# Attention heads: softmax weights left undivided, and each head's output multiplied by its rows' inverse sums

## The chip, the cores and the metric

The kernel runs on one core of a Trainium2 chip. The metric is the device time of one execution in microseconds. Engines are called PE (TensorE, matmuls), DVE (VectorE), ACT (ScalarE), POOL (GpSimd) and SP (SyncE, which issues the DMAs).

## What is computed

The reference is a network of several blocks on 512 tokens of width 1024, all in fp32. Three of its parts are attention: a block with 8 heads, which comes twice (two layers), and one with 16 heads of width 64. In each the part that matters here is a softmax over a row of scores, followed by the product with the values:

```python
s = jnp.where(mask[None, None], s, NEG_INF)
p = jax.nn.softmax(s, axis=-1).astype(v.dtype)
outs.append(jnp.einsum('bhqk,bhkd->bhqd', p, v[:, :kend]))
...
sc = jnp.einsum('bhqd,bhkd->bhqk', qb, kb).astype(jnp.float32) * scale + bias
sc = jnp.where(valid, sc, -jnp.inf)
p = jax.nn.softmax(sc, axis=-1).astype(vb.dtype)
return jnp.einsum('bhqk,bhkd->bhqd', p, vb)
```

## The kernel before

Activations lie feature by token (128 partitions of features, 512 tokens along the free dimension). Matmul operands are split into a high and a low fp32r half (`split`), so that a product takes three matmuls (`mm3`, L151 to L153). The stages follow one another: `mix` (heads and other branches), `ffn`, `mix`, `ffn`, `recurrent`, `mlp`, `attention`, `mlp`. The heads stand in `mix` (8 heads each) and in `attention` (16 heads), and both call `heads` with a list of items and a generator `filler`, which yields other matmuls (branches in `mix`, projections and output GEMMs in `attention`).

A head has four blocks of 128 queries, `qb` 0 to 3, with 128, 256, 384 and 512 keys. `scores` makes a block's scores in PSUM (L279 or L281, tag `ps_s`, two buffers), masks them, finds the row maximum (L291; in `attention` L295, which adds the bias too), and lets ACT take the exponent with the row sum as an accumulated by-product `sm` (L292, L297). Then it divides: DVE takes the reciprocal (L298), and the weights are multiplied by it row by row, the largest block on ACT (L300), the other three on DVE (L302). Here queries lie on the partitions, so the factor is one value per partition.

`turn` comes two blocks later (`depth` 2). It transposes a block of weights on PE (L314) into PSUM (tag `ps_t`, two buffers), and splits it (ACT L109, DVE L110). After the fourth block it multiplies by the values (L325, tag `ps_o`, one buffer): the two halves of the value operand give the two parts of the output in two halves of the partitions, so ACT copies one (L329, into `of`) and `done` adds it to the other (L523 in `mix`, L1030 in `attention`, where ACT and POOL then split it). Now queries lie along the free dimension. In `mix`, `of` has one buffer, shared with `prep`, which makes the queries of a later head (L509 writes `of`).

`prep` is called when block 1 of the head before has been scored, so just behind the `turn` of the fourth block of the head before that. In `attention` it calls `doubled` twice, each a product on DVE (`two`, L949) and four transposes into `ps_t` (L953); one is read by ACT and DVE as keys (`kh`, `kl`), one as queries (L963, L965).

`spread` (L199 to L205) is there before: it turns per-token columns into rows that are the same on all partitions, by transposing a column broadcast to 128x128 (L203, tag `ps_t`). The norms use it. The instructions of each engine are put in order ahead of time by a scheduler with a model of time; `high_priority` favours `scores` and `turn`, and `issue_after` holds instructions behind a given one.

Of the kernel before, what the change touches and what calls it, by code (L numbers as in the profile page):

```python
# [10 lines left out]
F32 = mybir.dt.float32  # L11
F32R = mybir.dt.float32r
I32 = mybir.dt.int32
AF = mybir.ActivationFunctionType
ALU = mybir.AluOpType
# [3 lines left out]
P = 128  # L19
# [47 lines left out]
class Net:  # L67
    def __init__(self, ctx, tc, d, out):
        self.tc, self.nc, self.d, self.out = tc, tc.nc, d, out
        self.small = ctx.enter_context(tc.tile_pool(name="small", bufs=1))  # L70
        self.base = ctx.enter_context(tc.tile_pool(name="base", bufs=1))
        self.psum = ctx.enter_context(tc.tile_pool(name="psum", bufs=1, space=PSUM))
        self.prm = self.small.tile([P, NPRM], F32, name="prm")

        self.half = self.small.tile([P, 32], F32, name="half")
        self.nc.gpsimd.memset(self.half[:, :16], -0.5)
        self.tab = self.small.tile([P, NTAB], F32, name="tab")
        self.uid = 0
        self.wide = 0
        self.after = []  # L80
# [189 lines left out]
    def scores(self, it, qb):  # L270
        nc = self.nc
        w = (qb + 1) * P
        s = self.ps("s")
        qs = slice(qb * P, w)
        q, k, rows = it["q"], it["k"], it.get("rows")
        if rows is None:

            for a, n in zip(k, range(2)):
                nc.tensor.matmul(out=s[:, :w], lhsT=q[:, qs], rhs=a[:, :w], start=n == 0, stop=n == 1)  # L279
        else:  # L280
            self.mm3(s[:, :w], (q[0][rows, qs], q[1][rows, qs]), (k[0][rows, :w], k[1][rows, :w]), True, True)  # L281
        bias = it.get("bias")
        if bias is None:
            nc.vector.memset(s[0:64, w - 64:w], NEG)
        else:
            pass
        m = self.t(self.small, "mx", 6, (P, 1))
        p = self.t(it["pool"], "p", it.get("p", 3))
        sm = self.t(self.small, "sm", 6, (P, 1))
        if bias is None:  # L290
            nc.vector.reduce_max(out=m, in_=s[:, :w], axis=AX, negate=True)  # L291
            nc.scalar.activation(out=p[:, :w], in_=s[:, :w], func=AF.Exp, bias=m, accum_out=sm)  # L292
        else:

            nc.vector.tensor_tensor_reduce(out=p[:, :w], in0=s[:, :w], in1=bias[:, 512 - w:], scale=-1.0,  # L295
                                           scalar=3e38, op0=ALU.add, op1=ALU.min, accum_out=m)
            nc.scalar.activation(out=p[:, :w], in_=p[:, :w], func=AF.Exp, bias=m, scale=-1.0, accum_out=sm)  # L297
        nc.vector.reciprocal(out=sm, in_=sm)  # L298
        if qb == 3:
            nc.scalar.activation(out=p, in_=p, func=AF.Copy, scale=sm)  # L300
        else:
            nc.vector.tensor_scalar(out=p[:, :w], in0=p[:, :w], scalar1=sm, scalar2=None, op0=ALU.mult)  # L302
        return p

    def turn(self, it, qb, p):

        nc = self.nc
        if qb == 0:
            it["pt"] = self.pair(it["pool"], "pt", 1, (P, 13, P))
        pth, ptl = it["pt"]  # L310
        pt = self.ps("t")
        for kb in range(qb + 1):
            ks = slice(kb * P, (kb + 1) * P)
            self.mark = nc.tensor.transpose(out=pt[:, ks], in_=p[:, ks], identity=self.c("ident"))  # L314

        dst = slice(qb, qb + 3 * qb + 1, 3)
        src = pt[:, :(qb + 1) * P].rearrange("p (k c) -> p k c", c=P)
        self.split((pth[:, dst], ptl[:, dst]), src)
        if qb == 3:

            o = self.ps("o")
            for kb in range(4):
                bs = slice(4 * kb, 4 * kb + 4 - kb)
                for pt in (pth, ptl):
                    nc.tensor.matmul(out=o[:, kb * P:], lhsT=it["v"](kb), rhs=pt[:, bs],  # L325
                                     start=kb == 0 and pt is pth, stop=kb == 3 and pt is ptl)
            a, b = (slice(0, 64), slice(64, 128))[::it["step"]]
            f = self.t(it["pool"], "of", it.get("of", 1))
            nc.scalar.activation(out=f[a], in_=o[b], func=AF.Copy)  # L329
            it["done"](o[a], f[a], a)  # L330

    def heads(self, items, filler, total, marks=None, hi=1000, depth=2):

# [29 lines left out]
        while pend:  # L363
            fill()
            turn()
            fill()
# [4 lines left out]
    def mix(self, l, gnext):  # L371
        nc, tc, d = self.nc, self.tc, self.d
        V, S_, G = nc.vector, nc.scalar, nc.gpsimd
# [4 lines left out]
        aout = [self.t(mp, "aout", 4) for _ in range(4)]  # L378
# [3 lines left out]
        with tc.tile_pool(name=f"att{l}", bufs=1, reuse_waits="tile") as ap:  # L382
# [28 lines left out]
            for j, S in enumerate((Sq, Sk)):  # L411
                for i in range(4):
                    nc.tensor.matmul(out=ps[:, 4 * j + i:4 * j + i + 1], lhsT=S[:, i * P:(i + 1) * P],
                                     rhs=self.c("inv", j, j + 1), start=True, stop=True)
# [25 lines left out]
            for i in range(4):  # L440
                f = vv[i // 2][:, i % 2 * 256:i % 2 * 256 + 256]
# [6 lines left out]
            for i in range(4):  # L448
                s = slice(i * 256, (i + 1) * 256)
                self.split((vn[0][:, s], vn[1][:, s]), vv[i // 2][:, i % 2 * 256:i % 2 * 256 + 256],  # L450
                           scale=r2[:, i:i + 1])
# [7 lines left out]
            for j in (6, 7):  # L459
                w = chunk(j)  # L460
# [28 lines left out]
            def values(j):  # L489
                wv = self.load(d["w_v"][l, j], P, pool=hp, tag="q", cap=384, raw_bufs=1, bufs=2)  # L490
                v = val[j] = self.t(ap, "v", 2, (P, 4, 4, 64), F32R)
                ps = self.ps("mm", (P, 4, P))
                for i in range(4):
                    ts = slice(i * P, (i + 1) * P)
                    self.mm3(ps[:, i], (ckv[0][:, ts], ckv[1][:, ts]), wv, True, True)
                self.split((v[:, :, 0::3], v[:, :, 1:3]), ps.rearrange("p i (h c) -> p i h c", c=64))
# [22 lines left out]
            def item(hd):  # L519
                j = hd // 2  # L520

                def done(o, f, rows):
                    V.tensor_tensor(out=aout[j][rows], in0=o, in1=f, op=ALU.add)  # L523
                    if hd in (0, 2, 4):
                        values(hd // 2 + 1)
                return dict(hd=hd, step=1 - hd % 2 * 2, rows=ALLP, pool=hp, prep=prep, done=done,
                            v=lambda kb: val[j][:, kb, hd % 2 * 2:hd % 2 * 2 + 2])
# [64 lines left out]
        with tc.tile_pool(name=f"gate{l}", bufs=1, reuse_waits="tile") as gp:  # L592
# [13 lines left out]
            for i in range(KT):  # L606
                m = self.t(gp, "m", 2)
                wo = None
                for n, nm in enumerate("cbda"):
# [4 lines left out]
                    if nm == "a":  # L614
                        w = self.load(d["w_br"][l, i, :, 768:], 512)
                    else:
                        wo = wo or self.load(d["w_br"][l, i, :, :768], 768)
                        w = (wo[0][:, n * 256:n * 256 + 256], wo[1][:, n * 256:n * 256 + 256])
# [284 lines left out]
    def attention(self, gnext):  # L903
        nc, tc, d = self.nc, self.tc, self.d
        V, S_, G = nc.vector, nc.scalar, nc.gpsimd
        xs, r = self.norm.xs, self.norm.r
        with tc.tile_pool(name="att", bufs=1, reuse_waits="tile") as ap:
            gqk = self.t(self.small, "rv", 1, (P, 4))[:, :1]
            V.scalar_tensor_tensor(out=gqk, in0=self.c("q_norm"), scalar=0.125, in1=self.c("k_norm"),
                                   op0=ALU.mult, op1=ALU.mult)  # L910
# [46 lines left out]
            def stacked(it, keys, queries, h):  # L957

                kk = self.t(ap, "kh", 3, dt=F32R), self.t(ap, "kl", 3, dt=F32R)
                self.split(kk, doubled(keys, h))  # L960
                q = self.t(ap, "q", 3, dt=F32R)
                ps = doubled(queries, h)
                S_.activation(out=q, in_=ps, func=AF.Copy, scale=gqk)  # L963
                lo = slice(64, P)
                V.scalar_tensor_tensor(out=q[lo], in0=ps[lo], scalar=gqk[lo], in1=q[lo].bitcast(F32), op0=ALU.mult,  # L965
                                       op1=ALU.subtract)
                it["k"], it["q"] = kk, q
# [46 lines left out]
            def item(hd):  # L1014
                group, h = groups[hd // 4], hd % 4

                def prep(it):
                    stacked(it, group[0][0], group[1][0], h)
                    b = bias[hd % 2]
                    nc.sync.dma_start(out=b[:, 256:], in_=d["bias"][hd])  # L1020
                    G.tensor_scalar(out=b[:, 256:], in0=b[:, 256:], scalar1=b[:, 256:257], scalar2=None,
                                    op0=ALU.subtract)
                    G.memset(b[0:64, 448:], NEG)
                    it["bias"] = b

                def done(o, f, rows):
                    j = hd // 2
                    if hd % 2 == 0:
                        os_[j] = self.pair(ap, "o", 6) if j < 6 else self.pair(ap, "k", 3)
                    V.tensor_tensor(out=f, in0=o, in1=f, op=ALU.add)  # L1030
                    self.split((os_[j][0][rows], os_[j][1][rows]), f, eng=G)

                return dict(p=4, step=1 - h % 2 * 2, pool=ap, prep=prep, done=done,
                            v=lambda kb: group[2][0][:, kb, h // 2, h % 2 * 2:h % 2 * 2 + 2])
# [177 lines left out]
```

## Time and profile before

| | us |
|---|---|
| median of 3 runs | 2803.64 |
| lowest and highest | 2803.21, 2806.1 |
| the profiled execution | 2796.84 |
| its span, first to last instruction | 2795.1 |
| PE busy in it | 2719.6 |
| DVE busy | 1570.9 |
| ACT busy | 1148.8 |
| POOL busy | 443.4 |

The span is what the profile's rows divide up; the profiled execution's own time is 1.7 us longer. Busy times of engines overlap. A row of waits names the engine and line that waited, then the line whose end released it, the time in total, how often, and the longest. The granted clock is 1.00 where PE runs at 2.4 GHz and 0.50 where it runs at 1.2 GHz.

### The profile page before, as it was taken

The numbers are of one execution on the slowest core, as the hardware profiler recorded it, in microseconds if no ns is written. First come the engines' busy times: TensorE is split into PE (matmuls) and PEld (weight loads), VectorE is DVE, ScalarE is ACT, GpSimd is POOL, SyncE is SP. The second block draws the span as 40 slices with busy tenths as digits, with TensorE's granted clock in tenths as the row PEclk, the third lists the DMA queues.
The fourth block names the chain that finished last, engine by engine and source line by source line (L and its number), as shares of the span: only waits on it lengthen the run. The fifth ranks groups of instructions, "written<-read, shape, count | busy, mean of one in ns | idle before, by whom it ended". The sixth has DMA issues, their size and how long they took to land.

```text
span 2795.1 us, 34599 instructions
## 1 busy us (share of the span) xinstructions
PE 2719.6 (97%) x13616; PEld 2304.5 (82%) x13616; DVE 1570.9 (56%) x2420; ACT 1148.8 (41%) x1894; POOL 443.4 (16%) x350
## 2 busy tenths in 40 slices
PE   8999999999999999999999998999999999899999
PEld 7778889888898778888888886888888888788887
DVE  5875555534467865456344478744444688744443
ACT  5553234322255543234222358433323567533222
POOL 5401110100004211101000100100004674200000
PEclk9999999999999999999999999999999999999999
DMA  4213232233322123242333322233223211133322
GB/s 152 63 46 98 92 106 89 91 100 96 96 89 95 48 64 98 93 132 64 95 96 100 92 93 78 77 106 97 94 96 97 72 63 63 63 98 92 105 95 87
DMA packets 77348, 249.70 MB, mean 89 GB/s; under 512 B 8577, under 2 KB 14593, under 8 KB 77185
## 3 DMA queue, kind: packets, MB, share of 16 engines
q1 hardware_dynamic: 77184, 247.49, 27.7%
q8 instruction: 107, 1.75, 0.3%
q14 instruction: 57, 0.46, 0.1%
HBM read 245.36 MB, written 2.10 MB: 89 GB/s over the span
## 4 chain that ended last, share of the span: by engine, by line
PE 88%; DVE 7%; ACT 3%; issue 1%; DMA 0%; POOL 0%; SPq 0%; DVEq 0%; ACTq 0%
PE ps_mm L151 16%; PE ps_mm L152 16%; PE ps_mm L153 16%; PE ps_s L152 9%; PE ps_s L151 9%; PE ps_s L153 9%; PE ps_o L153 3%; PE ps_o L152 3%; PE ps_o L151 3%; PE ps_o L325 1%; PE ps_t L314 1%; PE ps_s L279 1%; DVE xl L237 1%; ACT wh L109 1%; DVE S L214 0%
## 5 line engine op out<-in xcount | busy, mean ns | idle before, releaser
L109 ACT ACTIVATE wh<-raw 128x1024 fp32r<-128x1024 f32 (+3 forms) x403 | 411.8, 1024 | 1178.8 <-PE ps_mm L152 458.0
L110 DVE TENSOR_TENSOR wl<-raw,wh 128x1024 fp32r<-128x1024 f32 (+3 forms) x403 | 514.8, 1279 | 164.8 <-ACT wh L109 155.0
L151 PE MATMUL ps_mm<-xh,wh 128*128 128x512 f32 x1160 | 453.8, 392 | 7.3 <-ACT xh L112 6.8
L152 PE MATMUL ps_mm<-xl,wh 128*128 128x512 f32 x1160 | 453.2, 391 | 0.5 <-DVE xl L113 0.5
L153 PE MATMUL ps_mm<-xh,wl 128*128 128x512 f32 x1160 | 452.7, 391 | 0.0
L151 PEld LDWEIGHTS ps_mm<-xh,wh 128*128 128x128 f32 x1160 | 218.4, 188 | 53.8 <-ACT xh L112 6.8
L152 PEld LDWEIGHTS ps_mm<-xl,wh 128*128 128x128 f32 x1160 | 218.5, 188 | 45.4 <-DVE xl L113 1.0
L153 PEld LDWEIGHTS ps_mm<-xh,wl 128*128 128x128 f32 x1160 | 218.3, 188 | 45.4
L153 PE MATMUL ps_s<-xh,wl 128*128 128x512 f32 x552 | 215.5, 390 | 0.0
L151 PE MATMUL ps_s<-xh,wh 128*128 128x512 f32 x552 | 215.1, 390 | 0.0
L152 PE MATMUL ps_s<-xl,wh 128*128 128x512 f32 x552 | 214.8, 389 | 0.0
L151 PE MATMUL ps_mm<-hh,wh 128*128 128x512 f32 (+1 forms) x422 | 161.2, 382 | 0.0
L152 PE MATMUL ps_mm<-hl,wh 128*128 128x512 f32 (+1 forms) x422 | 160.9, 382 | 0.0
L153 PE MATMUL ps_mm<-hh,wl 128*128 128x512 f32 (+1 forms) x422 | 160.9, 382 | 0.0
L690 POOL TENSOR_TENSOR a<-a,rb 128x512 f32<-128x512 f32 x44 | 60.2, 1371 | 534.2 <-DVE a L689 534.2
L624 POOL TENSOR_TENSOR m<-m,g 128x512 f32<-128x512 f32 x48 | 62.6, 1304 | 433.4 <-DVE g L623 433.3
L153 PEld LDWEIGHTS ps_s<-xh,wl 128*128 128x128 f32 x552 | 103.6, 188 | 22.3 <-DVE wl L110 0.9
L151 PEld LDWEIGHTS ps_s<-xh,wh 128*128 128x128 f32 x552 | 103.7, 188 | 21.4
L152 PEld LDWEIGHTS ps_s<-xl,wh 128*128 128x128 f32 x552 | 103.6, 188 | 21.4
L151 PE MATMUL ps_s<-hh,wh 128*128 128x512 f32 (+1 forms) x308 | 117.0, 380 | 0.0
L152 PE MATMUL ps_s<-hl,wh 128*128 128x512 f32 (+1 forms) x308 | 116.8, 379 | 0.0
L153 PE MATMUL ps_s<-hh,wl 128*128 128x512 f32 (+1 forms) x308 | 116.8, 379 | 0.0
(462 smaller groups left out, 5858.4 us busy)
## 6 DMA issues: line engine op xcount, KB each, us to landing
raw<-in_w_in SPq DMA_DIRECT2D x96, 512.0 KB, 3.5
raw<-in_w_gu SPq DMA_DIRECT2D x88, 512.0 KB, 3.5
raw<-in_w_down SPq DMA_DIRECT2D x80, 512.0 KB, 3.5
raw<-in_w_up SPq DMA_DIRECT2D x64, 512.0 KB, 3.5
raw<-in_w_down SPq DMA_DIRECT2D x32, 448.0 KB, 3.3
raw<-in_w_qkv SPq DMA_DIRECT2D x24, 512.0 KB, 3.4
raw<-in_w_out SPq DMA_DIRECT2D x16, 512.0 KB, 3.5
raw<-in_a_w_in SPq DMA_DIRECT2D x16, 512.0 KB, 3.6
```

What stands on the lines that cost most here:

```text
L109: a = nc.scalar.activation(out=h, in_=src, func=AF.Copy)
L110: b = (eng or nc.vector).tensor_tensor(out=l, in0=src, in1=h.bitcast(F32), op=ALU.subtract)
L151: mm(out=ps, lhsT=a[0], rhs=b[0], start=first, stop=False)
L152: mm(out=ps, lhsT=a[0], rhs=b[1], start=False, stop=False)
L153: self.multiplied = mm(out=ps, lhsT=a[1], rhs=b[0], start=False, stop=last)
L237: lambda: self.nc.vector.scalar_tensor_tensor(out=l, in0=x, scalar=g, in1=h.bitcast(F32), op0=ALU.mult, op1=ALU.subtract))
L279: nc.tensor.matmul(out=s[:, :w], lhsT=q[:, qs], rhs=a[:, :w], start=n == 0, stop=n == 1)
L314: self.mark = nc.tensor.transpose(out=pt[:, ks], in_=p[:, ks], identity=self.c("ident"))
L325: nc.tensor.matmul(out=o[:, kb * P:], lhsT=it["v"](kb), rhs=pt[:, bs], start=kb == 0 and pt is pth, stop=kb == 3 and pt is ptl)
L624: G.tensor_tensor(out=m, in0=m, in1=g, op=ALU.add)
L690: G.tensor_tensor(out=a, in0=a, in1=rb, op=ALU.mult)
```

## The change

The weights stay undivided: reciprocal and scaling leave `scores`. The four row sums of a head lie in one tile of four columns (two buffers, for six of one column). When the head is done, one reciprocal of the four columns is taken in place, and `spread` transposes them into a PSUM tile of 128x512, whose every row holds the 512 inverse sums; `issue_after(end.ins)` holds these transposes behind the last matmul of the value product. `done` adds the two parts of the output into `of` and multiplies by the spread tile, 64 rows of 512. The tile `half` becomes 64 columns wide; only its first 16 are used, as before.

```diff
@@ -72,7 +72,7 @@
         self.psum = ctx.enter_context(tc.tile_pool(name="psum", bufs=1, space=PSUM))
         self.prm = self.small.tile([P, NPRM], F32, name="prm")
 
-        self.half = self.small.tile([P, 32], F32, name="half")
+        self.half = self.small.tile([P, 64], F32, name="half")
         self.nc.gpsimd.memset(self.half[:, :16], -0.5)
         self.tab = self.small.tile([P, NTAB], F32, name="tab")
         self.uid = 0
@@ -286,7 +286,9 @@
             pass
         m = self.t(self.small, "mx", 6, (P, 1))
         p = self.t(it["pool"], "p", it.get("p", 3))
-        sm = self.t(self.small, "sm", 6, (P, 1))
+        if qb == 0:
+            it["sm"] = self.t(self.small, "sm", 2, (P, 4))
+        sm = it["sm"][:, qb:qb + 1]
         if bias is None:
             nc.vector.reduce_max(out=m, in_=s[:, :w], axis=AX, negate=True)
             nc.scalar.activation(out=p[:, :w], in_=s[:, :w], func=AF.Exp, bias=m, accum_out=sm)
@@ -295,11 +297,6 @@
             nc.vector.tensor_tensor_reduce(out=p[:, :w], in0=s[:, :w], in1=bias[:, 512 - w:], scale=-1.0,
                                            scalar=3e38, op0=ALU.add, op1=ALU.min, accum_out=m)
             nc.scalar.activation(out=p[:, :w], in_=p[:, :w], func=AF.Exp, bias=m, scale=-1.0, accum_out=sm)
-        nc.vector.reciprocal(out=sm, in_=sm)
-        if qb == 3:
-            nc.scalar.activation(out=p, in_=p, func=AF.Copy, scale=sm)
-        else:
-            nc.vector.tensor_scalar(out=p[:, :w], in0=p[:, :w], scalar1=sm, scalar2=None, op0=ALU.mult)
         return p
 
     def turn(self, it, qb, p):
@@ -322,12 +319,16 @@
             for kb in range(4):
                 bs = slice(4 * kb, 4 * kb + 4 - kb)
                 for pt in (pth, ptl):
-                    nc.tensor.matmul(out=o[:, kb * P:], lhsT=it["v"](kb), rhs=pt[:, bs],
-                                     start=kb == 0 and pt is pth, stop=kb == 3 and pt is ptl)
+                    end = nc.tensor.matmul(out=o[:, kb * P:], lhsT=it["v"](kb), rhs=pt[:, bs],
+                                           start=kb == 0 and pt is pth, stop=kb == 3 and pt is ptl)
             a, b = (slice(0, 64), slice(64, 128))[::it["step"]]
             f = self.t(it["pool"], "of", it.get("of", 1))
             nc.scalar.activation(out=f[a], in_=o[b], func=AF.Copy)
-            it["done"](o[a], f[a], a)
+
+            nc.vector.reciprocal(out=it["sm"], in_=it["sm"])
+            with self.tc.issue_after(end.ins):
+                over = self.spread(it["sm"], range(4))
+            it["done"](o[a], f[a], over[a], a)
 
     def heads(self, items, filler, total, marks=None, hi=1000, depth=2):
 
@@ -519,8 +520,9 @@
             def item(hd):
                 j = hd // 2
 
-                def done(o, f, rows):
-                    V.tensor_tensor(out=aout[j][rows], in0=o, in1=f, op=ALU.add)
+                def done(o, f, over, rows):
+                    V.tensor_tensor(out=f, in0=o, in1=f, op=ALU.add)
+                    V.tensor_tensor(out=aout[j][rows], in0=over, in1=f, op=ALU.mult)
                     if hd in (0, 2, 4):
                         values(hd // 2 + 1)
                 return dict(hd=hd, step=1 - hd % 2 * 2, rows=ALLP, pool=hp, prep=prep, done=done,
@@ -1023,11 +1025,12 @@
                     G.memset(b[0:64, 448:], NEG)
                     it["bias"] = b
 
-                def done(o, f, rows):
+                def done(o, f, over, rows):
                     j = hd // 2
                     if hd % 2 == 0:
                         os_[j] = self.pair(ap, "o", 6) if j < 6 else self.pair(ap, "k", 3)
                     V.tensor_tensor(out=f, in0=o, in1=f, op=ALU.add)
+                    V.tensor_tensor(out=f, in0=over, in1=f, op=ALU.mult)
                     self.split((os_[j][0][rows], os_[j][1][rows]), f, eng=G)
 
                 return dict(p=4, step=1 - h % 2 * 2, pool=ap, prep=prep, done=done,
```

## Rows read from the trace of the kernel before

**Rows 1.** The page's busy times: busy us, share of the span, instructions

```profile
PE 2719.6 (97%) x13616; PEld 2304.5 (82%) x13616; DVE 1570.9 (56%) x2420; ACT 1148.8 (41%) x1894; POOL 443.4 (16%) x350
```

**Rows 2.** Stretches of the heads: length, busy PE PEld DVE ACT POOL, clock, DMA, GB/s

```profile
70.00:201.00 131.00, 121.11 (x614) 101.10 (x612) 99.10 (x225) 69.69 (x159) 30.39 (x22) 0.96 0.19 58
884.00:1016.00 132.00, 121.03 (x615) 99.44 (x614) 101.37 (x228) 71.26 (x162) 30.47 (x22) 0.98 0.19 58
2189.00:2432.00 243.00, 220.46 (x1565) 204.08 (x1562) 200.03 (x457) 160.74 (x364) 111.83 (x81) 0.98 0.20 65
```

**Rows 3.** PE's waits in attention: who, for what, us in total, times, longest

```profile
PE ps_t L314 <- DVE q L965: 7.5, 7, 2.7
PE ps_t L314 <- DVE kl L110: 4.9, 6, 1.4
```

**Rows 4.** A spread in the chain (start, us), and L203's records (min/median/max ns)

```profile
54.73 0.87 PE ps_t L203 x8
...
L203 PE MATMUL ps_t<-tab,r x64: 270/272/323, 28.5 to 2458.0; 128*128 128x128 f32 x64
```

**Rows 5.** PE's timeline in the mixes: start, us, instruction, [idle before <-releaser]

```profile
87.87 0.39 PE L151 MATMUL ps_s<-k1h,qh 128*128 128x256 f32 x1 [1.90 <-ACT p L292]
...
902.03 0.55 PE L314 MATMUL ps_t<-tab,p 128*128 128x128 f32 x3 [1.35 <-DVE p L302]
903.89 0.38 PE L151 MATMUL ps_s<-k1h,qh 128*128 128x256 f32 x1 [1.31 <-ACT p L292]
...
115.32 0.47 PE L151 MATMUL ps_mm<-cqh,wqh 128*128 128x512 f32 x1 [0.73 <-DVE of L509]
```

**Rows 6.** The stretches behind those first waits; the clock is third from last

```profile
88.00:96.00 8.00, 7.55 (x26) 6.02 (x27) 7.24 (x20) 5.97 (x16) 3.01 (x3) 0.57 0.13 48
904.00:908.00 4.00, 4.00 (x15) 3.15 (x15) 3.34 (x12) 3.98 (x11) 0.00 (x0) 0.57 0.28 96
```

**Rows 7.** L302: all runs; one and POOL beside it; its DVE time in two stretches

```profile
L302 DVE TENSOR_SCALAR p<-p,sm x96: 216/354/2481, 76.4 to 2417.1; 128x128 f32<-128x128 f32 x32, 128x256 f32<-128x256 f32 x32, 128x384 f32<-128x384 f32 x32
...
76.39 1.76 DVE L302 TENSOR_SCALAR p<-p,sm 128x128 f32<-128x128 f32 x1
...
75.22 5.20 POOL L144 TENSOR_TENSOR wl<-raw,wh 128x1024 fp32r<-128x1024 f32 x2
...
74.00:86.00 12.00, 3.00 (x3) 1.00 0.33 109
886.00:902.00 16.00, 3.73 (x3) 1.00 0.25 82
```

**Rows 8.** Busy DVE of L302, then of L298, summed over the three stretches

```profile
sum 506.00, DVE 54.99; mean DVE 18.33
...
sum 506.00, DVE 19.23; mean DVE 6.41
```

**Rows 9.** L523, the sum of a head's two output parts (min/median/max ns)

```profile
L523 DVE TENSOR_TENSOR aout<-ps_o,of x16: 664/688/695, 97.9 to 1014.0; 64x512 f32<-64x512 f32 x16
```

**Rows 10.** The end of a head in attention: timeline of ACT, DVE and PE

```profile
2330.61 0.72 ACT L300 ACTIVATE p<-p,sm 128x512 f32<-128x512 f32 x1
...
2333.56 0.60 ACT L329 ACTIVATE of<-ps_o 64x512 f32<-64x512 f32 x1
...
2334.25 0.67 DVE L1030 TENSOR_TENSOR of<-ps_o,of 64x512 f32<-64x512 f32 x1
2334.96 0.76 DVE L965 SCALAR_TENSOR_TENSOR q<-ps_t,rv,q 64x512 fp32r<-64x512 f32 x1
...
2335.77 0.44 PE L314 MATMUL ps_t<-tab,p 128*128 128x128 f32 x2 [1.74 <-DVE q L965]
```

**Rows 11.** PE behind the last head of the first mix and of attention

```profile
200.96 0.80 PE L151 MATMUL ps_s<-wfh,wh 128*128 128x512 f32 x1 [1.33 <-ACT wfh L109]
...
2431.11 0.97 PE L151 MATMUL ps_mm<-kh,wh 128*128 128x512 f32 x3 [2.12 <-ACT kh L109]
```

## The prediction

> **What bounds the kernel now.** First the page's busy times: TensorE (PE) is busy 97% of the span, VectorE (DVE) 56% [rows 1]. So PE sets the time, and an edit counts only by what it adds to PE's stream or takes from PE's idle time. Then the busy time by stage, in the three stretches where `heads` runs: two of 8 heads (131 and 132 us) and one of 16 (243 us) [rows 2]. There PE is idle for 9.9, 11.0 and 22.5 us, 43.4 us together, and DVE is busy for 400.5 of 506 us: the one place of the kernel where DVE comes close to PE. All that the change touches lies in these stretches. The list of waits of the attention stage says what PE waits for: 12.4 us in 13 waits of the weight transposes (L314) for a `ps_t` buffer that DVE has not yet read out (L965, L110) [rows 3]. It does not wait for the division there.
>
> **The spread, added to PE.** Each of 32 heads gets four transposes in which a column of `sm` is the loaded operand, as in L203 now. In the chain of work eight of those take 0.87 us, 0.109 each, though each has a record of 272 ns, since neighbours overlap [rows 4]. 32 x 4 x 0.109 = **+13.9 us** of PE. The bounds are 0.109 and the whole record, 34.8 us; I take the pitch, because a head's four follow each other just as those eight do.
>
> The Trainium skill (TensorE: Matmul & The Clock Gate, Part 4: PE-mode transpose) gives about 275 ns for a 128x128 transpose inside a kernel and says that a copy out of PSUM comes after it: a rule against this change. By it the spread would be estimated at 35 us; the records here agree with its figure, the pitch does not. It is a rival below.
>
> **The division, removed.** 96 scalings on DVE (L302), 32 on ACT (L300) and 128 reciprocals (L298) go; over the three stretches L302 and L298 are busy for 55.0 and 19.2 us [rows 8]. In come 32 reciprocals of four columns, an estimate of 0.15 each from L298's mean (19.2/128), since even L302's 128x128 takes no more than 0.216 at its shortest [rows 7], and 32 products of a PSUM tile and an SBUF tile of 64x512, the shape of L523, 0.69 [rows 9]: 26.9 us. DVE loses 47.3 of 400.5 us, 12%. That is worth nothing by itself; it is worth what PE waits for.
>
> *At the start of the two mix stages* it is worth most. There DVE is full, and L302 stretches: one of 128x128 elements took 1.76 us while POOL ran L144, where the shortest takes 0.216 [rows 7]. In the 12 us before the first wait, L302 alone holds DVE for 3.00 us, and for 3.73 us in the second mix [rows 7]. PE then waits 1.90 us in the first mix, 1.35 and 1.31 in the second [rows 5], less than what DVE gets back, so I take all 4.6 us off. After these waits the granted clock falls: 0.57 over 8 us and over 4 us [rows 6], between the levels of 2.4 and 1.2 GHz; work at 0.57 of full speed loses 0.43 of its time, 5.2 us. Both go with the waits: **-9.8 us**. If DVE only loses its time to POOL elsewhere, this is zero.
>
> The Trainium skill (SBUF — State Buffer, Who interferes with whom) has VectorE and GpSimd take one shared port pair in turn, the first holding it for its whole instruction; single-source VectorE work in a two-port mode and work with two SBUF inputs are held up, work with one SBUF input outside those modes is not. The stretched L302 agrees, and by that rule the new product, with one input in PSUM, is never stretched: L523 stays between 664 and 695 ns in all 16 runs [rows 9].
>
> *In attention* I scale: DVE has 12% less work, so 12% of the 12.4 us of waits, **-1.5 us**; the bounds are 0 and half of them, 6.2.
>
> **Where the spread is free.** Where PE waits for DVE soon after a head's value product, the spread fills the wait. In attention the 13 waits lie in some 8 of 16 heads: 8 x 0.435 = 3.5 us. In the mixes four waits of 0.7 to 1.6 us come right behind a value product (the first is the last row of [rows 5]), 1.7 us. Behind the last head of each stage PE waits 1.3, 1.3 and 2.1 us for ACT (the first and the last in [rows 11]), 1.3 us. Together **-6.5 us**. If those waits vanish first, this cover is gone and up to 6.5 us come back, but then the waits are gone too.
>
> **The product, added to DVE's queue.** It stands behind L523 or L1030. Queued behind it are, in the mixes, the reads of `ps_mm` for which PE has the four waits just named (L509 needs DVE, and the single `of` buffer that now frees one product later): 4 x 0.69 = 2.8 us. In attention it is L965: at 2334 us L1030 runs just ahead of L965, for which PE waits 1.7 us [rows 10]. There are 7 such waits [rows 3], 4.8 us; but L300's 0.72 leaves the ACT queue ahead of L963, which L965 needs too [rows 10], and I count half of it back: 2.5. The last head's output is on the way to the next GEMM: 0.7. Together **+5.8 us**, bounds 0 (the scheduler puts the product behind L965) and 8.3. Nothing else queues: no DMA is issued or moved, and POOL's split of the output (ACT's too) starts 0.7 us later with nearly a head's time to spare.
>
> **A fifth user of `ps_t`.** No row of before shows a spread between heads, so its wait is bounded. Its two-buffer tag now holds a tile from the spread until the product; in attention that is the seventh allocation of a head beside four turns and two of `doubled`. Below zero is excluded, since one more holder frees nothing. Above, each of 16 heads waits one product longer, 11.0 us. Today the waits for `kl` cost 4.9 us in 16 heads [rows 3]; the spread comes while filler work is at hand and its buffer is not needed by the very next transposes, so I take less than half of that, **+2.0 us**. The reciprocal costs PE nothing: all it needs is there before the last block's transposes, and the value product covers it (without that cover its 0.15 per head, 4.8 us).
>
> **The sum**: 13.9 - 9.8 - 1.5 - 6.5 + 5.8 + 2.0 = **+3.9 us**. The durations come from the profiled execution, 2796.84 us (span 2795.1 and 1.7 around it), so it would become 2800.7; the median of the runs is 6.8 above that execution, and carried over to it the forecast is 2803.64 + 3.9 = **2807.5 us**, no difference that can be told. Its own range is 2798 to 2809.2.
>
> **Rivals.** *DVE's relief carries further.* For it: DVE holds 82% of attention and the waits are all on it [rows 2, 3]. Half of the 12.4 us goes (4.7 more than counted), `ps_t` costs nothing (2.0) and the product falls behind the late reads (5.8): 3.9 - 12.5 = -8.6, 2795.0 us. Against it: just ahead of L965 stands L1030 and no division [rows 10].
>
> *The spread holds `ps_t`* (slower). In attention the tile is held from the end of the value product through ACT's copy, the sum and the product. L329 follows L300 with three microseconds between at 2330 to 2334 us [rows 10], so the hold is over 4 us where a turn's is one or two, and the turns of the next head queue for the other buffer. Its price is 11.0 instead of 2.0, and the 3.5 us of free spread in attention are lost as well: 3.9 + 12.5 = +16.4, 2820.0 us. It decides from about 0.23 us per head on, (5.6 - 3.9 + 2.0)/16. Against it: filler matmuls lie between most turns.
>
> *The change doesn't do what it says for DVE*: POOL's L144 then stretches the next SBUF work (L550, L110) in place of L302, and the waits at the starts stay. +3.9 + 9.8 = +13.7, 2817.3 us. For it: POOL's work is unchanged. Against it: the two longest stretches sit on L302.
>
> *Transposes at their whole record*: if each holds PE for 272 ns, 34.8 in place of 13.9: +24.8, 2828.4 us. The chain row speaks against it [rows 4]. By the skill's page above it would be the case.
>
> **How the numbers follow.** What a measurement of this kernel can tell from no change is about 0.2%, 5.6 us. Forecast 0.42; DVE's relief 0.25; `ps_t` 0.20; POOL's stretch moving on 0.08; whole records 0.05. So faster 0.25, same 0.42, slower 0.33. The range reaches past the relief's 2795.0 for its bounds, and just past the `ps_t` case: 2789 to 2822; it leaves out whole records and the ends of the others.
>
> **What the profile after would show.** 128 more transposes under L203's place, at a pitch near 0.11. No scalings under the old L302 and L300; DVE's busy time about 47 us lower, ACT's 23 (32 x 0.72) lower. No PE wait of over a microsecond in the first 16 us of either mix, and a granted clock of 1.0 there; if those waits stand, term two was wrong. In attention the waits of the turns for DVE should stay near 12 us; if they rise by 5 or more, or the spread itself waits, the `ps_t` rival holds; if they halve, the relief does. A product that runs well after its sum would show the reciprocal or the spread late. The forecast would be wrong altogether if the order of PE's work outside the three stretches changed.

## The result and the profile after

The changed kernel takes 2850.25 us (median of 4 runs, 2848.07 to 2853.91), the kernel before 2803.43 beside it (2797.48 to 2806.1): a ratio of 1.0185, 95% interval 1.017 to 1.0199. It is 47 us slower, where no difference was forecast and the range ended at 2822.

The busy times of the changed kernel, from its page (columns as in [rows 1]):

```profile
PE 2758.1 (97%) x13744; PEld 2336.9 (82%) x13744; DVE 1541.5 (54%) x2260; ACT 1128.4 (40%) x1862; POOL 445.7 (16%) x350
```

DVE and ACT have less to do, as meant; PE has 38.5 us more. The stretches of the heads in the changed kernel, the answer to [rows 2] (length, busy PE PEld DVE ACT POOL, clock, DMA, GB/s):

```profile
70.00:203.50 133.50, 125.03 (x647) 102.82 (x645) 91.60 (x186) 64.60 (x152) 31.70 (x22) 0.98 0.18 57
884.00:1024.00 140.00, 130.06 (x659) 106.83 (x657) 96.50 (x193) 66.42 (x156) 33.22 (x23) 0.96 0.18 56
2199.60:2488.50 288.90, 245.07 (x1627) 226.57 (x1625) 187.69 (x377) 152.78 (x348) 111.17 (x81) 0.91 0.17 55
```

Attention stands out: 46 us longer, PE idle for 43.8 us instead of 22.5, and a granted clock of 0.91 instead of 0.98. To compare kernels, three stages are cut at the same instructions in each: a mix from the first product with `rb` to its last gate, attention from the first transpose of `two` to the last split into `kh`. Each is read in steps of 5 us: PE's idle time; what its work lost to a granted clock under 1 (busy time times one minus the clock); and the rest, the work itself. The three parts add up to the length.

| us: length = idle + clock + work | first mix | second mix | attention |
|---|---|---|---|
| before | 378.2 = 10.3 + 6.9 + 360.9 | 371.8 = 11.1 + 4.0 + 356.6 | 241.6 = 21.9 + 3.6 + 216.1 |
| changed | 380.6 = 9.6 + 5.4 + 365.5 | 378.5 = 10.9 + 7.0 + 360.6 | 288.1 = 43.2 + 21.5 + 223.4 |

So attention lost 46.5 us: 7.3 of work, 21.3 of idle time, and 17.9 that PE's work lost to a lower clock. The mixes lost 2.4 and 6.7. Each length is read from one execution, and the two of this table lie 57 us apart where the medians lie 47 apart. Over all runs here, attention that divides as before takes 241.6 to 246.1 us (six executions), and the mixes with the old division 375.3 and 378.2, then 371.8 and 373.6 (two executions); differences of this size say nothing. PE's waits in attention say for what (PE and line, what was waited for, us in total, times, longest), the answer to [rows 3]:

```profile
PE ps_t L955 <- DVE of L1033: 14.8, 8, 2.4
PE ps_t L955 <- DVE kl L110: 9.4, 4, 2.8
PE ps_t L955 <- DVE rs_v L184: 8.3, 2, 4.6
PE ps_t L311 <- DVE kl L110: 5.8, 2, 3.3
```

Before, the weights' transposes (old L314, now L311) waited. Now it is mostly `doubled`'s transposes (old L953, now L955), and always the four of the queries: in each of the 14 heads in which keys and queries follow a spread. In eight they are released by the product L1033, a line that the change added (14.8 us). In the other six the split of the keys (`kl`) has just ended, also in the two that the list puts down to `rs_v`: there `kl` ends at 2297.20 and 2368.77, 0.15 us before PE starts. One head of the eight, in the timeline (start, us, instruction, idle before it and releaser):

```profile
2329.05 0.40 PE L322 MATMUL ps_o<-pth,v 128*128 128x512 f32 x1
...
2330.28 0.62 PE L203 MATMUL ps_t<-tab,sm 128*128 128x128 f32 x4
2330.53 0.59 ACT L326 ACTIVATE of<-ps_o 64x512 f32<-64x512 f32 x1 [1.66 <-PE ps_o L322]
2330.73 0.60 PE L955 MATMUL ps_t<-tab,two 128*128 128x128 f32 x4
2331.16 0.68 DVE L1032 TENSOR_TENSOR of<-ps_o,of 64x512 f32<-64x512 f32 x1
2332.37 0.68 DVE L1033 TENSOR_TENSOR of<-ps_t,of 64x512 f32<-64x512 f32 x1
2333.19 0.63 PE L955 MATMUL ps_t<-tab,two 128*128 128x128 f32 x4 [1.86 <-DVE of L1033]
```

The spread is done at 2330.9, but its `ps_t` buffer is free only at 2333.1, behind ACT's copy, the sum and the product. One head of the six, where the queries start when the keys are split and the product is still running:

```profile
2349.25 0.69 DVE L110 TENSOR_TENSOR kl<-ps_t,kh 128x512 fp32r<-128x512 f32 x1
2349.97 0.69 DVE L1033 TENSOR_TENSOR of<-ps_t,of 64x512 f32<-64x512 f32 x1
2350.09 0.63 PE L955 MATMUL ps_t<-tab,two 128*128 128x128 f32 x4 [1.87 <-DVE kl L110]
```

So the spread and the keys hold the two buffers of `ps_t`, and the queries wait until DVE has read out one of them. Before, PE had another order; a head there:

```profile
2327.12 0.60 PE L953 MATMUL ps_t<-tab,two 128*128 128x128 f32 x4
...
2328.99 0.39 PE L325 MATMUL ps_o<-pth,v 128*128 128x512 f32 x1
...
2330.36 0.62 PE L953 MATMUL ps_t<-tab,two 128*128 128x128 f32 x4
```

In all 14 heads the keys were transposed ahead of the value product, and the queries came behind it; in this one the keys were split from 2329.4 to 2330.7, while it ran. In the changed kernel the keys come behind value product and spread in all 14: the spread stands ahead of them in the program, in the same tag, and is held behind the value product. PE takes its instructions in the order given, so all that is queued behind the queries waits with them.

### The profile page after: what moved, and what is told of

Read it like the earlier page. It is cut to its first block, busy times and chain, and to the rows that moved or that the text cites. A ratio compares the mean times of both kernels' runs of the same rounds, so it can differ in the third digit from the quotient of the medians.

```text
span 2852.1 us, 34694 instructions
## 1 busy us (share of the span) xinstructions
PE 2758.1 (97%) x13744; PEld 2336.9 (82%) x13744; DVE 1541.5 (54%) x2260; ACT 1128.4 (40%) x1862; POOL 445.7 (16%) x350
## 4 chain that ended last, share of the span: by engine, by line
PE 88%; DVE 8%; ACT 3%; issue 1%; POOL 0%; DMA 0%; ACTq 0%; DVEq 0%
PE ps_mm L151 16%; PE ps_mm L152 16%; PE ps_mm L153 16%; PE ps_s L152 9%; PE ps_s L153 9%; PE ps_s L151 9%; PE ps_o L153 3%; PE ps_o L152 3%; PE ps_o L151 3%; PE ps_o L322 1%; PE ps_t L311 1%; PE ps_s L279 1%; DVE two L951 1%; DVE xl L237 1%; DVE wl L110 1%
```

## The experiments

Four explanations were open: the hold of the spread's buffer and its place in that order; the product in DVE's queue; the spread's own time on PE; the order that the scheduler makes once the scalings are gone. Where an expectation names a theory by a letter, the numbers beside it say what it expects. The fences show the lines of an edit that matter, not all of it. All times are medians beside runs of the kernel before; lengths are of the three stages of the table.

**What the division itself is worth.** Sums are taken and nothing divides: reciprocal, spread and product are left out, so the output lacks the division.

```diff
-            nc.vector.reciprocal(out=it["sm"], in_=it["sm"])
-            with self.tc.issue_after(end.ins):
-                over = self.spread(it["sm"], range(4))
-            it["done"](o[a], f[a], over[a], a)
+            it["done"](o[a], f[a], None, a)
```

> The changed kernel with reciprocal, spread and product taken out: the weights stay undivided and the outputs too (the division is left out). Theory S (the spread sits in the ps_t slot that the next head's keys would have had, and the queries' transposes wait for the product): with no spread the attention stretch goes back to at most its 243 us of before, and what the removed scaling is worth shows alone: by the prediction's terms 9.8 + 1.5 us off, 2792 us; with nothing gained 2803. Rival O (the lost time comes from the order that the scheduler makes once the scalings are gone): it stays near 2840. Rival W (it is the work of spread and product on PE and DVE): also about 2792 to 2803, so this run tells O from the other two.

Measured: 2781.06 us, ratio 0.9934 [0.992, 0.9949]. The mixes go to 366.8 (4.9 + 1.4 + 360.4) and 364.2 (6.9 + 1.5 + 355.8), attention stays at 241.3. So the division costs 11.4 and 7.6 us in the mixes, nearly all of it idle time and lower clock, and nothing in attention: a total below the 2792 that was expected. The scalings' share of DVE's load is no reason for PE's waits in attention, which stand without the division too (21.4 us of idle time), and the order without scalings is no cause of the loss.

**The mixes alone.** Attention divides as before, the mixes are as changed.

```diff
+        if bias is not None:
+            nc.vector.reciprocal(out=sm, in_=sm)
+            ...
```

> Only the 16 heads of the two mix stages get the change, the 16 of attention divide their weights as before. All theories that put the loss into attention: the stages before attention came 10.6 us later in the changed kernel, so about 2814 us, and 36 us of the 47 go. If the loss were spread over all heads alike (half in the mixes): 2827.

Measured: 2808.78 us, ratio 1.0033 [1.0021, 1.0046]; 379.3, 378.3 and 245.1. Of the 47 us, some 10 come with the mixes, the rest with attention.

**The spread in another tag.** In attention alone the spread takes a buffer of `ps_mm` (three of them) instead of `ps_t`; spread, sum and product stay.

```diff
-                over = self.spread(it["sm"], range(4))
+                over = self.spread(it["sm"], range(4), "t" if it.get("bias") is None else "mm")
```

> The changed kernel, with the spread of the 16 attention heads in the three-buffer tag ps_mm instead of ps_t; work and number of instructions are the same. Theory S: the queries' transposes no longer wait for the product, attention falls from 289 us to about 243 + 7 for the spread itself, total 2811 us (2805 to 2820 with some waits of the projections for ps_mm). Rival W (work): stays at 2845 to 2855. Rival O (order): stays within 10 us of 2850.

Measured: 2810.79 us, ratio 1.0042 [1.0027, 1.0057]. Attention is back at 247.0 (20.2 + 3.7 + 223.1): the spread's work is all that is left. Neither that work nor the product in DVE's queue can then be the cause of the other 39 us; the buffer is. PE transposes the keys ahead of the value product again, in all 14 heads, and its largest waits in that stage are for splits of weights, keys and queries:

```profile
PE ps_o L322 <- DVE ptl L110: 7.0, 7, 1.8
PE ps_t L311 <- DVE kl L110: 5.4, 3, 3.2
PE ps_t L311 <- DVE q L967: 4.1, 5, 1.6
```

**The order, with a short hold.** The kernel before, with four transposes of a constant into `ps_t` behind each value product of attention. ACT reads one element per partition, behind its copy of the output; there is no product.

```diff
+            if it.get("bias") is not None:
+                with self.tc.issue_after(end.ins):
+                    over = self.spread(self.c("ident"), range(4))
+                nc.scalar.activation(out=self.half[:, 16:17], in_=over[:, 0:1], func=AF.Copy)
             it["done"](o[a], f[a], a)
```

> The kernel before, with its scalings, plus in each of the 16 attention heads four transposes of a constant column into ps_t behind the value product, read at once by ACT in one column; no product, no reciprocal of four, nothing computed from it. Work of the spread alone: 16 x 0.44 = 7 us, 2806 to 2808. Theory H: little more, since the hold is short: 2808 to 2818. Rival R: the seventh slot alone brings most of attention's 46 us: 2825 to 2845.

Measured: 2829.13 us, ratio 1.0103 [1.0088, 1.0118]; attention 276.3 (38.9 + 12.0 + 225.4): within what rival R expected. Even a buffer that ACT reads with one instruction of 0.17 us costs 34.7 us there, 9.3 of it work and 25.4 idle time and clock. That is not quite an order without a hold: four times the queries still waited for ACT's read. The changed kernel's other 11.8 us come with the longer hold and the product; a run for the hold alone is lacking, since a kernel in which ACT copies the spread to SBUF for the product didn't fit (107 KB per partition, 105.97 left). What is late now are the keys' readers, for which the weights (L314 here) wait:

```profile
PE ps_t L314 <- DVE kl L110: 21.2, 12, 2.9
PE ps_t L957 <- DVE two L953: 4.6, 2, 2.4
PE ps_t L957 <- ACT half L333: 3.7, 4, 2.2
```

In [rows 3] that first wait was 4.9 us in 6. Here too the keys come behind value product and spread in all 14 heads, so they are split later, and the first block's weights, which come next, wait for that.

**Keys and queries first.** The changed kernel, in attention with `prep` called ahead of the turn of the fourth block instead of behind it, so that keys and queries don't follow the spread.

```diff
+                if early and qb == 1 and n + 1 < len(items):
+                    items[n + 1]["prep"](items[n + 1])
                 if len(pend) > depth:
                     turn()
-                if qb == 1 and n + 1 < len(items):
+                if not early and qb == 1 and n + 1 < len(items):
                     items[n + 1]["prep"](items[n + 1])
```

> The changed kernel, with prep of the next but one head called just ahead of the turn of a head's fourth block in attention, instead of just behind it: keys and queries take their ps_t slots before the spread does. Theory S: the waits of the queries' transposes for the product (14.8 us named so, 32.5 us with those for kl and rs_v) go, and some come back on the turn of the next head's second block, which now shares the slot with the spread: 2812 to 2825 us. Rivals W and O: 2840 to 2855.

Measured: 2849.52 us, ratio 1.0176 [1.0161, 1.0192]; attention 282.5 (44.4 + 15.9 + 222.2). This expectation failed: no wait for the product was left, but the weights of the fourth block now come behind keys and queries and wait for the keys' split, more often and longer:

```profile
PE ps_t L311 <- DVE kl L110: 30.4, 13, 4.7
PE ps_t L957 <- DVE two L953: 8.6, 2, 5.2
```

This reordering within two buffers moved the wait; it didn't remove it.

**All spreads in `ps_mm`.** The tag `ps_mm`, tried above in attention alone, in the mixes too.

> The changed kernel with the spread of all 32 heads in ps_mm. Against the run with attention's alone in ps_mm (2811): if ps_t costs in the mixes too, where transposes wait for the product for 0.8 us and behind the last block for 2.0 us of a stage, with the clock that follows, 5 to 10 us go: 2800 to 2806. If not, or if the branches then wait for ps_mm: 2811 or more.

Measured: 2806.76 us, ratio 1.0026 [1.0016, 1.0036]; 381.2 (10.4 + 6.7 + 364.1), 374.9 (10.8 + 4.6 + 359.5) and 245.2. In the mixes the tag decides little: 0.6 us more in the first, 3.6 less in the second.

**Division on ACT.** The kernel before, with every scaling of the mixes on ACT. This takes L302 off DVE there without a spread.

```diff
-        if qb == 3:
-            nc.scalar.activation(out=p, in_=p, func=AF.Copy, scale=sm)
+        if qb == 3 or bias is None:
+            nc.scalar.activation(out=p[:, :w], in_=p[:, :w], func=AF.Copy, scale=sm)
```

> The kernel before, but in the two mix stages ACT scales all four blocks of weights (24 scalings per stage move from DVE to ACT); attention as before. No division gave 18 us in the mixes. If what was gained there is DVE's time and its stretches beside POOL, most comes here too, less ACT's 8 us per stage where PE waits for ACT: 2784 to 2794 us. If the gain came from the shorter chain from exponent to transpose, none of it comes: 2797 to 2803.

Measured: 2805.44 us, ratio 1.0017 [1.0008, 1.0026]; 379.2, 374.4 and 243.1. Moving these scalings from DVE to ACT gives nothing, as expected if the scaling counts as one more step between scores and turn; that ACT's added load ate a gain was not excluded.

**Spread and product one turn later.** Reciprocal, spread and product of a head stand behind the first turn of the next head; first in all stages, then in the mixes with attention as before.

```diff
-            it["done"](o[a], f[a], over[a], a)
+            rest = it["done"](o[a], f[a], a)
...
+            self.owed.append(owe)
+        elif qb == 0 and self.owed:
+            self.owed.pop()()
```

> All 32 heads divide at the output, but reciprocal, spread, product (and attention's split of the output) come one turn later, behind the transposes of the next head's first block; the sum of the two parts stays where it was, in the mixes straight into its final tile, so of is not held longer. Work as in the changed kernel. Theory R (the slot's place in the two-slot ring is what costs: ahead of keys and queries it makes them, and the weights behind them, wait in a row): here the spread comes when keys and queries are through and is held only for one product, so attention costs its 7 us of spread and little more, 249 to 254 us instead of 288; in the mixes 3.5 us each on top of the run without a division, 370 and 368 us: 2795 to 2804 in all. Rival N (a seventh slot costs about 25 us wherever it stands, as the constant one did): 2822 to 2835.

> The same later spread in the two mix stages alone; attention divides its weights as before. If ring and of are what ate the 18 us that no division gave in the mixes: those less 7 us of spread are left, 2788 to 2794 us, faster than both kernels. If the product's time in DVE's queue ate them, wherever it stands: 2803 to 2810, as with the mixes alone changed.

Measured: 2812.95 us, ratio 1.0047 [1.0032, 1.0062], with 380.1, 378.0 and 246.8; and 2810.3, ratio 1.0037 [1.0023, 1.0051], with 382.7, 378.0 and 243.4. In attention this restores the old order for keys and queries, and the loss shrinks to 5.2 us, less than the 7.0 of added work: a second way to take the cause away, with the tile still in `ps_t`, and here too the keys are ahead of the value product. In the mixes it gains nothing, so both total times lie above what was expected (2795 to 2804, 2788 to 2794).

**Where the mixes' gain goes.** Two more kernels divide as before in attention. In the first, all sums of a mix lie in one tile of 32 columns; one reciprocal, the eight spreads and eight products stand behind the heads, in the gate stage. In the second, each head makes its spread as changed, but ACT reads one element of it and the product is left out, so the mixes' output lacks the division.

```diff
+            V.reciprocal(out=sums, in_=sums)
+            for hd in range(8):
+                over = self.spread(sums[:, 4 * hd:4 * hd + 4], range(4))
+                f = aout[hd // 2][slice(64, 128) if hd % 2 else slice(0, 64)]
+                V.tensor_tensor(out=f, in0=over[slice(64, 128) if hd % 2 else slice(0, 64)], in1=f, op=ALU.mult)
             br = {}
```

> Attention divides as before. In the two mixes the weights stay undivided; all sums of a stage go to one 128x32 tile, and one reciprocal, eight spreads in ps_t and eight products in place on aout stand behind the heads, in the gate stage, just ahead of the split of aout. Theory A (the spread and the product inside the heads' stretch ate what the missing division gives): the mixes gain as with the division left out, 18.9 us, and give back only the spreads' own PE time, 2 x 8 x 0.435 = 7 us, partly under waits: 2783 to 2792 us, the mix stretches near 367 and 364 us plus at most 7 each. Theory B (a product costs what a division cost, wherever it stands): 2800 to 2810.

> Attention divides as before. In the mixes the weights stay undivided and each head makes its reciprocal and its spread as in the changed kernel, but the product is left out: one element per partition of the spread is copied by ACT at once, so the output lacks the division in the two mixes. If the product in the queue of DVE ate the gain of the missing division: the stretches go to 370 and 368 us (division left out, 366.8 and 364.2, plus 3.5 of spread), the time to 2786 to 2792 us. If the spread, its place among the transposes and its slot did: the stretches stay near 379 and 377, the time near 2805 to 2810.

Measured: behind the heads 2786.35 us (2785.21 to 2790.2; 2799.52 before), ratio 0.9952 [0.9937, 0.9967], with 370.3 (5.1 + 0.0 + 365.2), 367.4 (6.3 + 1.4 + 359.7) and 243.0. It is faster than both kernels. Without the product 2798.42 us, ratio 0.9996 [0.9987, 1.0006], with 374.0 (6.8 + 2.9 + 364.3), 373.7 (10.2 + 3.1 + 360.4) and 246.1. The first mix's stretch of the kernel with all behind the heads, as the first of [rows 2]:

```profile
70.00:192.00 122.00, 118.92 (x633) 100.08 (x632) 85.18 (x174) 67.10 (x154) 32.47 (x22) 1.00 0.20 62
```

PE is idle for 3.1 us of it, against 9.9 in 131, and the clock is 1.00. Against the kernel without division, spread and product cost 3.5 and 3.2 us behind the heads. Inside them the spread with its buffer costs 7.2 and 9.5, and the product 5.3 and 4.6 more (the mixes alone, less the kernel without product). These are single executions, so the split is good to some 3 us. The work is the same in both places (365.2 and 365.1 in the first mix): what is lost inside is idle time and clock. The spread's idle time there is again a `ps_t` wait of the next weights, on ACT's read, up to 1.2 us; with the product it is the last row of this list of the changed kernel's waits from 70 to 215 us:

```profile
PE ps_t L311 <- DVE ptl L110: 2.3, 2, 2.0
...
PE ps_t L311 <- DVE aout L525: 0.8, 2, 0.5
```

Which of the two shares in the mixes is the order and which the hold was not taken apart, and why moving the spread by one turn or to `ps_mm` didn't help there stays open.

## Why the prediction was wrong, point by point

**The fifth user of `ps_t`** is the step that failed: +2.0 us, at most 11.0. It measured 39.2 in attention (46.5 less the spread's 7.3 of work). Three things were missing. The bound was one more product per head, as if only the hold could cost; the kernel with the slot alone shows 25.4 with no product and mostly a short hold. The order was not worked out: a spread that stands in the program between turn 3 and keys, in their tag and held behind the value product, takes the keys from ahead of that product to behind it, and then spread and keys hold both buffers when the queries come. "Its buffer is not needed by the very next transposes" holds for the keys alone; PE was ready for the queries 0.4 us after the spread's end (2331.3 and 2330.9 in the first timeline above). And no clock was counted: of the 39.2, 17.9 are work at a lower clock. The rival "the spread holds `ps_t`" named the tag, the stage, the sign and the hold, but not the order, and took its price from the same bound, so 2820.0 was still 30 short.

**The spread's own time** was right: +13.9 us forecast, 4.6 + 4.0 + 7.3 = 15.9 measured, 0.124 us a transpose. The records still say 272:

```profile
L203 PE MATMUL ps_t<-tab,sm x128: 272/273/435, 91.9 to 2485.4; 128*128 128x128 f32 x128
```

So whole records (34.8 us) are excluded. What the Trainium skill (TensorE: Matmul & The Clock Gate, Part 4: PE-mode transpose) gives for bf16 inside a kernel, about 275 ns, is the length of the fp32 record here; four in a row start closer together, as in [rows 4].

**The starts of the mixes** did not give -9.8; idle time and clock of the two mixes together changed by +0.6. What was foreseen as a rival is what the trace shows: beside POOL's L144 other instructions on DVE are stretched (first mix, then second; POOL's L144, then DVE beside it).

```profile
83.58 2.39 POOL L144 TENSOR_TENSOR wl<-raw,wh 128x1024 fp32r<-128x1024 f32 x1 [0.88 <-ACT wh L141]
83.74 2.27 DVE L554 TENSOR_TENSOR tt<-tt,tab 64x16 f32<-64x16 f32 x1
...
902.41 2.44 POOL L144 TENSOR_TENSOR wl<-raw,wh 128x1024 fp32r<-128x1024 f32 x1 [3.18 <-ACT wh L141]
902.66 2.23 DVE L554 TENSOR_TENSOR tt<-tt,tab 64x16 f32<-64x16 f32 x1
```

The median of L554 is 0.17 us. PE still waits at both starts, 1.5 us before 87.7 and 2.8 before 906.5; without division, spread and product it waits 1.7 at the first. The prediction also took the two longest stretches to sit on L302 (2.48 at most, [rows 7]). A longer one stood just ahead of the first wait before, beside L144 too, and was no division:

```profile
83.55 2.52 DVE L550 TENSOR_SCALAR tt<-tt,prm 64x512 f32<-64x512 f32 x1
```

The clock of the first start did come back (1.00, where [rows 6] has 0.57), but it is 1.00 there too in the kernel with the slot alone, whose mixes divide as before, so the change need not be the reason; over both mixes the loss went from 10.9 to 12.4 us:

```profile
88.00:96.00 8.00, 7.60 (x41) 5.92 (x40) 7.84 (x19) 6.36 (x17) 3.31 (x3) 1.00 0.17 60
```

The Trainium skill's rule on the shared port (SBUF — State Buffer, Who interferes with whom) held in both directions: work with two SBUF inputs was stretched, and the product with one input in PSUM was not (669 to 695 ns in 16 runs in the mixes, one of them, at 127.2, beside L144).

**Relief of DVE.** In attention -1.5 was forecast; the kernel without division shows -0.3, which can't be told from nothing. The size of the relief was overrated too: DVE's busy time fell by 29.4 us, not 47.3. The sums of its records fell by 44.7 (1664.3 to 1619.6 over all groups), but neighbouring records overlap, so a sum over records counts more than DVE's busy time does (1664.3 against 1570.9 before). ACT fell by 20.4, near the 23 foreseen.

**Cover.** -6.5 was counted. With the buffer's cost out of the way (spread in `ps_mm`), attention's idle time is 1.7 lower than before; that of the mixes is 0.9 lower in the changed kernel. By these traces some 2.6 us were free, not 6.5.

**The product in DVE's queue** was put at +5.8, 2.8 of it in the mixes. There it is 5.3 + 4.6 = 9.9. In attention it is at most 11.8 (the changed kernel less the slot alone), through `ps_t` and not through DVE's queue: in `ps_mm` the product costs nothing to be seen.

**Terms that were balanced against each other.** In the mixes the division is worth 19.0 us, more than the 9.8 that the prediction took; but the same heads pay 26.6 us for spread and product (379.3 - 366.8 and 378.3 - 364.2). The sign in the mixes hung on where the new steps stand, which the prediction did not vary.

## What to carry to other kernels

Before adding a tile to a tag of few buffers, write down the order of its users on the engine with it, and see what each now comes behind and which readouts it waits for. The price is that chain in every pass, and part of it again as a lower clock, not only the new tile's own hold. In the mixes a step taken out of the heads became cheap: gather per-head factors in one tile and apply them behind the last head, as the version at 2786.35 us does. And time taken from a busy engine is worth what another engine waits for it, which leaving the step out altogether shows before its replacement is written.

## What the runs showed of the hardware

Stalls of PE that recur with the heads, most of them of 1 to 3 us, came with a loss of half to nearly as much again in clock: in attention 21.3 us more of idle time with 17.9 us more lost to a granted clock of 0.91 on average, and in the kernel with the slot alone 17.0 with 8.4. The 2.2 us before 2315.8 in the changed kernel were followed by a granted clock of 0.58 from 2316 to 2320, between the levels of 2.4 and 1.2 GHz; the 1.9 us before 2333.2 by 1.00 from 2332 to 2340. Where the stalls went (spread in `ps_mm`), the clock loss was 3.7, as before. And four transposes that load a broadcast column, with records of 273 ns, take 0.12 us each of PE's time.
